# PSUM's eight banks laid out anew for the recurrence stage of a two-layer gated encoder

## The chip, the cores and the metric

One core of a Trainium2 chip runs the whole program. The metric is the device time in microseconds from launch to end, the median of several executions. The engines that matter are TensorE (PE, with its weight loads as PEld), VectorE (DVE), ScalarE (ACT), GpSimd (POOL) and the DMA queues. PSUM, into which matmuls write, has eight banks of 128 x 512 float32.

## The reference

A sequence of 512 tokens of width 1024 goes through two layers. In each, one big projection of the normalised input feeds five mixers, and a gated merge adds their outputs up:

```python
for l in range(DEPTH):
    p = jnp.einsum('bsd,dc->bsc', h, w_in[l])
    pa, pb, pc, pd, pm = split_last(p, mixer_sizes)
    o_a = mixer_dilated(pa, table_a)
    o_b = mixer_rwkv(pb, shift_mu[l], ...)        # a recurrence over 512 steps, both directions
    o_c = mixer_axial_gqa(pc, c_qnorm_g[l], c_knorm_g[l], row, col)
    o_d = mixer_diff(pd, d_lambda[l], d_subln_g[l], table_d, l)
    o_m = mixer_memory(pm, mem, w_mem_kv[l])
    y = gated_merge(h, (o_a, o_b, o_c, o_d, o_m), w_branch[l], w_gate[l], b_gate[l])
    out = jnp.einsum('bsd,de->bse', y, w_out[l])
    h = layer_norm(alpha * h + out, ln_g[l], ln_b[l])

# gated_merge: for each of the five branches i
proj = jnp.einsum('bsc,cd->bsd', o, w_branch[start:start + wdt])
gate = jax.nn.sigmoid(jnp.einsum('bsd,de->bse', h, w_gate[:, i*d:(i+1)*d]) + b_gate[i*d:(i+1)*d])
terms.append(gate * proj)
```

Four mixers are attentions. mixer_rwkv is a linear recurrence with a 64 x 64 state for each of eight heads, run forwards and backwards.

## The kernel before

All products are made in float32 as three matmuls of a high and a low part (`gemm3_steps`, L145 to L152), so a projection of one 128-wide block is 8 steps of 3 matmuls with 512 columns. Weights are loaded raw (L125) and split by ACT (L135) and DVE (L136), each part with two buffers.

A layer has three stages. In the **attention stage** (L410 to L702, SBUF pool `att`) the heads of the four attention mixers run one after the other: projections into PSUM tile pg, scores into psc, softmax on DVE and ACT, transposes into pt, the weighted sums into po, and the gate `silu2` (L347), again a projection into pg that ACT (L352) and DVE (L353) read. Finished heads are stored to DRAM (scr_o). The last PSUM read of a head is L492. In the **recurrence stage** (L705 to L1109, SBUF pool `rw`) the mixer rwkv is computed in chunks of 64 steps, for four pairs of heads and two directions: eight units, each with an `early` part (k, r and v are projected by `mixed`, L730, into pg, once for a pair; decay, masks, small products) and a `late` part (a triangular solve on DVE, L949 to L966, then the chain over the chunks, L1035 to L1043), and for a pair a `finish`, which has a `silu2` too. Before the units, `mixed` projects blocks 12 and 13. `mixed` reads its bank three times: ACT (L734), then DVE twice (L735, L736). In the **output stage** (L1112 to L1148, SBUF pool `out`) the rwkv branch is merged with gates in psc and branch products in pg, and the product with w_out and the layer norm follow.

The gates and branch products of the other four branches are **fill**: a generator (`branch_steps`, L369, through `fill`, L395) that is pulled step by step. The attention stage pulls 0.7 steps after each score of the second mixer and 0.3 after each of the last (L621, L698); the recurrence pulls one step at each of its yields (L1106), and what is left is run at its end (L1108). For one block, fill makes the gate product in a tile pf (8 steps), ACT takes its tanh (L379), the branch product goes into another tile pf (4 steps, or 2 for the last branch), and DVE multiplies (L385, or L387 and L389).

The eight banks are one pool for the whole kernel: pg two, pf one, psc two, pt two, and one for po and pm. A tile that is asked for while all banks of its name are taken waits until one has been read for the last time.

The order of the instructions on each engine is not the order of the text. A scheduler places them before the run: it prefers what stands earlier in the text, and where that isn't ready, takes later work whose inputs and buffers are. It is fixed then, and each engine works through its list in order. A pool of tiles has a beginning and an end in the text, and a pool that is opened where another was closed takes over its memory.

Of the kernel before, what the change touches and what calls it, by code (L numbers as in the profile page):

```python
# [9 lines left out]
F32 = mybir.dt.float32  # L10
# [5 lines left out]
PSUM = bass.MemoryType.PSUM  # L16
# [36 lines left out]
def encoder_kernel(ctx: ExitStack, tc: tile.TileContext, x, mem, ln_in, rel_bias, w_in, par, w_up, a_up,  # L53
# [3 lines left out]
    const = ctx.enter_context(tc.tile_pool(name="const", bufs=1))  # L57
    big = ctx.enter_context(tc.tile_pool(name="big", bufs=1))
    wp = ctx.enter_context(tc.tile_pool(name="wp", bufs=1))
    pp = ctx.enter_context(tc.tile_pool(name="pp", bufs=1, space=PSUM))  # L60

    def ps_g():
        return pp.tile([128, 512], F32, name="pg", tag="pg", bufs=2)

    def ps_f():
        return pp.tile([128, 512], F32, name="pf", tag="pf", bufs=1)

    def ps_s():
        return pp.tile([128, 512], F32, name="psc", tag="psc", bufs=2)

    def ps_t():
        return pp.tile([128, 512], F32, name="pt", tag="pt", bufs=2)

    def ps_o():
        return pp.tile([128, 512], F32, name="po", tag="pm", bufs=1)

    def ps_m():
        return pp.tile([128, 512], F32, name="pm", tag="pm", bufs=1)

    mm = nc.tensor.matmul  # L80
    act = nc.scalar.activation
    tt = nc.vector.tensor_tensor
# [89 lines left out]
    def split2(hi, lo, src, scale=None):  # L172

        if scale is None:
            nc.scalar.copy(hi, src)  # L175
            tt(lo, src, f(hi), ALU.subtract)  # L176
        else:
            act(hi, src, AF.Copy, scale=scale)
            stt(lo, src, scale, f(hi), ALU.mult, ALU.subtract)

    def rsqrt(v):


        n = v.shape[-1]
        y = wp.tile([128, 8], F32, name="rsy", tag="rsy", bufs=2)[:, :n]
        a = wp.tile([128, 8], F32, name="rsa", tag="rsa", bufs=2)[:, :n]
        ts(y.bitcast(I32), v.bitcast(I32), -0.5, float(0x5f3759df), ALU.mult, ALU.add)

        stt(a, y, 0.375 ** 0.5, v, ALU.mult, ALU.mult)
        tt(a, a, y, ALU.mult)  # L190
        stt(a, a, 1.25 / 0.375 ** 0.5, a, ALU.subtract, ALU.mult)
        stt(y, a, 1.875, y, ALU.add, ALU.mult)
        stt(a, y, -0.5, v, ALU.mult, ALU.mult)
        tt(a, a, y, ALU.mult)
        stt(v, a, 1.5, y, ALU.add, ALU.mult)
# [27 lines left out]
    def layernorm(pool, xts, gb, hT, dst):  # L223
        n = len(xts)
        mv = pool.tile([128, 4, 2], F32, name="lnmv", tag="lnmv", bufs=2)
        for j, (xt, t) in enumerate(xts):
            st = pool.tile([128, 2, 6], F32, name="lnst", tag="lnst", bufs=2)
            for i in range(2):
                nc.vector.bn_stats(out=st[:, i, :], in_=xt[:, i * 512:(i + 1) * 512])
            nc.vector.bn_aggr(out=mv[:, j], in_=st)  # L230
        ts(mv[:, :n, 1], mv[:, :n, 1], 1e-5, None, ALU.add)
        rsqrt(mv[:, :n, 1])
        for j, (xt, t) in enumerate(xts):

            for sn in (slice(0, DM),) if hT is not None else (slice(0, 512), slice(512, DM)):
                stt(xt[:, sn], xt[:, sn], mv[:, j, 0:1], gb[:, 0, sn], ALU.subtract, ALU.mult)
                stt(xt[:, sn], xt[:, sn], mv[:, j, 1:2], gb[:, 1, sn], ALU.mult, ALU.add)
                nc.sync.dma_start(out=dst[t * 128:(t + 1) * 128, sn], in_=xt[:, sn])
            if hT is None:
                continue  # L240
            for j2 in range(2):
                ps = ps_t()
                for i in range(4):
                    nc.tensor.transpose(ps[:, i * 128:(i + 1) * 128],
                                        xt[:, (4 * j2 + i) * 128:(4 * j2 + i + 1) * 128], ident)
                sl = slice(t * 128, (t + 1) * 128)
                pv = ps.rearrange("p (k t) -> p k t", k=4)
                split2(hT[:, 0, 4 * j2:4 * j2 + 4, sl], hT[:, 1, 4 * j2:4 * j2 + 4, sl], pv)
# [75 lines left out]
    for l in range(L):  # L324
# [85 lines left out]
        with tc.tile_pool(name=f"att{l}", bufs=1) as at:  # L410
# [83 lines left out]
            def gated(of, g2, out=False):  # L494
                tt(of, of, g2, ALU.mult)
                return finish_o(at, of, out)
# [29 lines left out]
            for hp in range(4):  # L526
# [21 lines left out]
                for i in range(2):  # L548
                    b = load_bias(2 * hp + i)
                    p4 = []  # L550
                    for qb in range(4):
                        ps = ps_s()
                        score(ps, q, k, i, qb, S)
                        p, _ = softmax(ps, S, b[:, 384 - 128 * qb:896 - 128 * qb])
# [55 lines left out]
            for b in range(4):  # L610
# [3 lines left out]
                for i in range(2):  # L614
                    p4 = []
                    for qb in range(4):
                        ps = ps_s()
                        score(ps, q, (kh, kl), i, qb, S, g)
                        p, _ = softmax(ps, S)
# [6 lines left out]
                t = gated(of, g2, True)  # L626
# [3 lines left out]
            with tc.tile_pool(name=f"attd{l}", bufs=1) as ad:  # L630
# [12 lines left out]
                for h in range(4):  # L643
# [23 lines left out]
                    po = ps_o()  # L667
# [9 lines left out]
                    t = finish_o(at, o, True)  # L677
# [3 lines left out]
            with tc.tile_pool(name=f"attm{l}", bufs=1) as am:  # L681
                kv = am.tile([128, 4, 256], F32, name="kvm", tag="kvm")
                nc.sync.dma_start(out=kv, in_=scr_kv[l].rearrange("b p t -> p b t"))
                for b in range(2):
# [6 lines left out]
                    for i in range(2):  # L691
                        p4 = []
                        for qb in range(4):
                            ps = ps_s()
                            score(ps, q, k, i, qb, 256)
                            p, _ = softmax(ps, 256, None, (DVE, ACT)[qb % 2])
# [4 lines left out]
                    t = gated(of, g2, True)  # L701
                    spill(4, b, t)  # L702


        with tc.tile_pool(name=f"rw{l}", bufs=1) as rp:  # L705
            def T(n, shape, bufs=1, dt=F32):
                return rp.tile(shape, dt, name=n, tag=n, bufs=bufs)
# [401 lines left out]
                pass  # L1109


        with tc.tile_pool(name=f"out{l}", bufs=1) as op:  # L1112
            yh, wo, z = [], [], []
            last = l == L - 1

            def load_z(t):
                zt = op.tile([128, DM], F32, name="z", tag="z", bufs=4)
                nc.sync.dma_start(out=zt, in_=scr_h[t * 128:(t + 1) * 128, :])
                z.append((zt, t))

            def done(db, yt):
                hi = big.tile([128, S], F32R, name="yh", tag="y", bufs=8)
                lo = op.tile([128, S], F32R, name="yl", tag="yl", bufs=8)
                split2(hi, lo, yt, 0.5)
                yh.append((hi, lo))
                t = op.tile([128, 2, DM], F32R, name="wo", tag="wo", bufs=8)
                for o in range(0, DM, 512):
                    raw = wp.tile([128, 512], F32, name="wrawr", tag="wrawr", bufs=2)
                    nc.sync.dma_start(out=raw, in_=w_out[l, db * 128:(db + 1) * 128, o:o + 512])
                    split2(t[:, 0, o:o + 512], t[:, 1, o:o + 512], raw)  # L1130
                wo.append(t)

            gb = load_gb(op, lnp[l])
            for _ in branch_steps(1, None, 4, done, "r", op, 2):
                pass
            for t in range(4):
                load_z(t)
            if not last:
                hT = new_hT()
            for t in range(4):  # L1140
                sl = slice(t * 128, (t + 1) * 128)
                for n in range(2):
                    ps = ps_g()
                    sn = slice(n * 512, (n + 1) * 512)
                    gemm3(ps, [(yh[k][0][:, sl], yh[k][1][:, sl], wo[k][:, 0, sn], wo[k][:, 1, sn]) for k in range(8)])
                    stt(z[t][0][:, sn], z[t][0][:, sn], ALPHA, ps, ALU.mult, ALU.add)
                if t:
                    layernorm(op, z[(0, 2, 3)[t - 1]:t + 1], gb, None if last else hT, out if last else scr_h)  # L1148


def _bucket(rel):
# [121 lines left out]
```

## Time and profile before

| | us |
|---|---|
| median of 3 executions (2313.76 to 2317.56) | 2314.18 |
| the profiled execution | 2311.92 |
| its span, first to last instruction | 2310.1 |

| engine | busy us | share of the span | instructions |
|---|---|---|---|
| PE (matmul) | 2206.5 | 96% | 13056 |
| PEld (weight load) | 1690.5 | 73% | 13056 |
| DVE | 1733.0 | 75% | 4236 |
| ACT | 1273.5 | 55% | 2785 |
| POOL | 60.9 | 3% | 119 |

Busy times are sums of an engine's instructions. Matmuls overlap, so a busy PE is not PE at its peak. The mean granted TensorE clock is 0.991 of full speed. In the rows below, times are microseconds from the span's start, `out<-in` names the tiles, L149 is a line of the kernel, a bracket tells how long an engine was idle before an instruction and what ended that, and a wait is put down to what came last.

### The profile page before, as it was taken

The numbers are of one execution on the slowest core, as the hardware profiler recorded it, in microseconds if no ns is written. First come the engines' busy times: TensorE is split into PE (matmuls) and PEld (weight loads), VectorE is DVE, ScalarE is ACT, GpSimd is POOL, SyncE is SP. The second block draws the span as 40 slices with busy tenths as digits, with TensorE's granted clock in tenths as the row PEclk, the third lists the DMA queues.
The fourth block names the chain that finished last, engine by engine and source line by source line (L and its number), as shares of the span: only waits on it lengthen the run. The fifth ranks groups of instructions, "written<-read, shape, count | busy, mean of one in ns | idle before, by whom it ended". The sixth has DMA issues, their size and how long they took to land.

```text
span 2310.1 us, 36289 instructions
## 1 busy us (share of the span) xinstructions
PE 2206.5 (96%) x13056; PEld 1690.5 (73%) x13056; DVE 1733.0 (75%) x4236; ACT 1273.5 (55%) x2785; POOL 60.9 (3%) x119
## 2 busy tenths in 40 slices
PE   6999999999999999999999999999999999999998
PEld 5877777777677777776877777777677777777676
DVE  7676886576889797965567778766778979878455
ACT  3555666675655565544235656666675646555440
POOL 0000000000000000000000000000000000000000
PEclk9999999999999999999999999999999999999999
DMA  7733123332222221315334321232312222222350
GB/s 261 230 95 86 64 76 96 105 95 80 73 79 70 93 77 60 108 51 190 101 116 104 94 64 62 94 99 83 114 60 92 74 65 94 72 93 67 100 180 37
DMA packets 112612, 222.58 MB, mean 96 GB/s; under 512 B 13304, under 2 KB 23288, under 8 KB 112048
## 3 DMA queue, kind: packets, MB, share of 16 engines
q1 hardware_dynamic: 102000, 196.14, 26.5%
q0 software_dynamic: 10432, 24.12, 4.1%
q8 instruction: 103, 1.69, 0.3%
q14 instruction: 77, 0.63, 0.1%
HBM read 188.71 MB, written 28.36 MB: 94 GB/s over the span
## 4 chain that ended last, share of the span: by engine, by line
PE 53%; issue 17%; DVE 17%; ACT 7%; DMA 5%; POOL 0%; SPq 0%; DVEq 0%; POOLq 0%; ACTq 0%
PE pg L150 7%; PE pg L151 7%; PE pg L149 7%; PE pf L149 5%; PE pf L150 4%; PE pf L151 4%; PE psc L443 3%; DVE pr L959 2%; DVE W L961 2%; PE po L488 2%; PE pt L469 2%; DVE wlof L136 1%; PE psc L151 1%; PE psc L150 1%; PE psc L149 1%
## 5 line engine op out<-in xcount | busy, mean ns | idle before, releaser
L150 PE MATMUL pg<-hT,whir 128*128 128x512 f32 (+1 forms) x912 | 366.0, 401 | 0.5 <-DVE hT L176 0.5
L149 PE MATMUL pg<-hT,whir 128*128 128x512 f32 (+1 forms) x912 | 364.4, 400 | 1.9 <-DVE q L424 1.6
L151 PE MATMUL pg<-hT,wlor 128*128 128x512 f32 (+1 forms) x912 | 364.3, 399 | 1.7 <-DVE wlor L136 1.7
L136 DVE TENSOR_TENSOR wlor<-wrawr,whir 128x512 fp32r<-128x512 f32 x240 | 163.7, 687 | 123.2 <-ACT whir L135 114.5
L135 ACT CAST whif<-wrawf 128x512 fp32r<-128x512 f32 (+1 forms) x272 | 164.6, 606 | 149.9 <-PE pf L150 87.4
L135 ACT CAST whir<-wrawr 128x512 fp32r<-128x512 f32 x240 | 147.5, 618 | 178.4 <-PE pg L150 111.9
L149 PE MATMUL pf<-hT,whif 128*128 128x512 f32 x512 | 223.0, 435 | 8.9 <-DVE y L385 5.0
L136 DVE TENSOR_TENSOR wlof<-wrawf,whif 128x512 fp32r<-128x512 f32 (+1 forms) x272 | 181.6, 669 | 48.3 <-ACT whif L135 43.1
L150 PE MATMUL pf<-hT,whif 128*128 128x512 f32 x512 | 208.3, 407 | 0.0
L151 PE MATMUL pf<-hT,wlof 128*128 128x512 f32 x512 | 207.7, 406 | 0.0
L151 PEld LDWEIGHTS pg<-hT,wlor 128*128 128x128 f32 x912 | 172.2, 189 | 40.6 <-DVE wlor L136 4.2
L149 PEld LDWEIGHTS pg<-hT,whir 128*128 128x128 f32 x912 | 172.4, 189 | 38.8 <-ACT whir L135 2.6
L150 PEld LDWEIGHTS pg<-hT,whir 128*128 128x128 f32 x912 | 172.2, 189 | 37.8 <-issue 3.6
L176 DVE TENSOR_TENSOR pT<-pt,pT 128x512 fp32r<-128x512 f32 x176 | 114.2, 686 | 36.3 <-ACT pT L175 34.9
L175 ACT CAST pT<-pt 128x512 fp32r<-128x512 f32 x176 | 94.6, 588 | 63.7 <-PE pt L469 62.6
L149 PEld LDWEIGHTS pf<-hT,whif 128*128 128x128 f32 x512 | 97.5, 190 | 41.2 <-DVE gt L387 10.7
L469 PE MATMUL pt<-cst,p 128*128 128x128 f32 x704 | 118.6, 273 | 0.0
L151 PEld LDWEIGHTS pf<-hT,wlof 128*128 128x128 f32 x512 | 97.3, 190 | 22.4 <-issue 1.6
L959 DVE TENSOR_TENSOR pr<-W,U 128x60 f32<-128x60 f32 (+24 forms) x496 | 103.8, 209 | 11.9
L150 PEld LDWEIGHTS pf<-hT,whif 128*128 128x128 f32 x512 | 98.0, 191 | 18.9 <-issue 3.9
L961 DVE TENSOR_TENSOR W<-W,pr 128x60 f32<-128x60 f32 (+24 forms) x496 | 102.8, 207 | 10.8
L469 PEld LDWEIGHTS pt<-cst,p 128*128 128x128 f32 x704 | 89.7, 141 | 27.3 <-DVE p L460 2.9
(324 smaller groups left out, 4836.9 us busy)
## 6 DMA issues: line engine op xcount, KB each, us to landing
wrawr<-in_w_in_dram SPq DMA_DIRECT2D x224, 256.0 KB, 2.8
wrawf<-in_w_gate_dram SPq DMA_DIRECT2D x160, 256.0 KB, 2.8
o<-scr_o POOLq DMA_DIRECT2D x28, 512.0 KB, 4.5
wrawf<-in_w_branch_dram SPq DMA_DIRECT2D x48, 256.0 KB, 2.7
bias<-scr_toe SPq DMA_DIRECT2D x24, 448.0 KB, 3.3
scr_o<-os SPq DMA_DIRECT2D x20, 512.0 KB, 3.1
wrawf<-in_w_in_dram SPq DMA_DIRECT2D x32, 256.0 KB, 3.2
wrawr<-in_w_out_dram SPq DMA_DIRECT2D x32, 256.0 KB, 3.0
```

The costliest lines, as they stand in the source:

```text
L135: nc.scalar.copy(hi, raw)
L136: tt(lo, raw, f(hi), ALU.subtract)
L149: mm(ps, ah, bh, start=(i == 0), stop=False)
L150: mm(ps, ah, bl, start=False, stop=False)
L151: mm(ps, al, bh, start=False, stop=(i == n - 1))
L175: nc.scalar.copy(hi, src)
L176: tt(lo, src, f(hi), ALU.subtract)
L443: mm(ps[:, :nk], q[:, i, sl], part[:, i if g is None else g, :nk], start=(j == 0), stop=(j == 1))
L469: nc.tensor.transpose(pt[:, qb * 128:(qb + 1) * 128], p4[qb][:, kb * 128:(kb + 1) * 128], ident)
L488: mm(po, vwin(kb), pT[:, b, :], start=(kb == 0 and b == 0), stop=(kb == nkb - 1 and b == 1))
L959: tt(pr, W[:, t8, s:s + 1].to_broadcast([128, nt, n]), U[:, s:s + 1, rsl].to_broadcast([128, nt, n]), ALU.mult)
L961: tt(W[:, t8, rsl], W[:, t8, rsl], pr, ALU.add)
```

## The change

The single PSUM pool becomes a sequence of pools, closed and opened by a helper `banks`. Around the recurrence of each layer the layout is pg one, pf two; before it and after it, pg two and pf one, as it was. psc, pt and the bank for po and pm keep their numbers. The functions that hand out tiles (`ps_g`, `ps_f` and the others) take them from the pool that is open when they are called. The generator of the fill is not touched: it is resumed under whichever pool is open.

```diff
@@ -57,26 +57,38 @@
     const = ctx.enter_context(tc.tile_pool(name="const", bufs=1))
     big = ctx.enter_context(tc.tile_pool(name="big", bufs=1))
     wp = ctx.enter_context(tc.tile_pool(name="wp", bufs=1))
-    pp = ctx.enter_context(tc.tile_pool(name="pp", bufs=1, space=PSUM))
+
+    pool = {}
+
+    def banks(name, **bufs):
+
+        if pool:
+            pool["p"].__exit__(None, None, None)
+        pool["p"] = tc.tile_pool(name=name, bufs=1, space=PSUM)
+        pool["t"], pool["n"] = pool["p"].__enter__(), bufs
+
+    def ps_of(tag, name):
+        return pool["t"].tile([128, 512], F32, name=name, tag=tag, bufs=pool["n"][tag])
 
     def ps_g():
-        return pp.tile([128, 512], F32, name="pg", tag="pg", bufs=2)
+        return ps_of("pg", "pg")
 
     def ps_f():
-        return pp.tile([128, 512], F32, name="pf", tag="pf", bufs=1)
+        return ps_of("pf", "pf")
 
     def ps_s():
-        return pp.tile([128, 512], F32, name="psc", tag="psc", bufs=2)
+        return ps_of("psc", "psc")
 
     def ps_t():
-        return pp.tile([128, 512], F32, name="pt", tag="pt", bufs=2)
+        return ps_of("pt", "pt")
 
     def ps_o():
-        return pp.tile([128, 512], F32, name="po", tag="pm", bufs=1)
+        return ps_of("pm", "po")
 
     def ps_m():
-        return pp.tile([128, 512], F32, name="pm", tag="pm", bufs=1)
-
+        return ps_of("pm", "pm")
+
+    banks("pp", pg=2, pf=1, psc=2, pt=2, pm=1)
     mm = nc.tensor.matmul
     act = nc.scalar.activation
     tt = nc.vector.tensor_tensor
@@ -702,6 +714,7 @@
                     spill(4, b, t)
 
 
+        banks(f"pr{l}", pg=1, pf=2, psc=2, pt=2, pm=1)
         with tc.tile_pool(name=f"rw{l}", bufs=1) as rp:
             def T(n, shape, bufs=1, dt=F32):
                 return rp.tile(shape, dt, name=n, tag=n, bufs=bufs)
@@ -1109,6 +1122,7 @@
                 pass
 
 
+        banks(f"pp{l}", pg=2, pf=1, psc=2, pt=2, pm=1)
         with tc.tile_pool(name=f"out{l}", bufs=1) as op:
             yh, wo, z = [], [], []
             last = l == L - 1
@@ -1146,6 +1160,7 @@
                     stt(z[t][0][:, sn], z[t][0][:, sn], ALPHA, ps, ALU.mult, ALU.add)
                 if t:
                     layernorm(op, z[(0, 2, 3)[t - 1]:t + 1], gb, None if last else hT, out if last else scr_h)
+    pool["p"].__exit__(None, None, None)
 
 
 def _bucket(rel):
```

## Rows read from the trace of the kernel before

**Rows 1.** Stages: busy us (instructions) of PE, PEld, DVE, ACT, POOL; clock; DMA.
```profile
506.00:528.00 22.00, 21.31 (x110) 16.39 (x109) 18.31 (x46) 17.97 (x48) 0.00 (x0) 1.00 0.21 73
541.00:1057.00 516.00, 499.10 (x3699) 373.24 (x3698) 419.21 (x1132) 293.14 (x698) 7.02 (x13) 0.99 0.24 75
1667.00:2184.00 517.00, 500.19 (x3704) 374.27 (x3703) 420.78 (x1136) 294.78 (x700) 7.02 (x13) 0.99 0.24 75
```

**Rows 2.** Timeline of PE, two matmuls in a row: start, duration, line, tiles.
```profile
540.05 0.39 PE L150 MATMUL pg<-hT,whir 128*128 128x512 f32 x1
540.28 0.39 PE L151 MATMUL pg<-hT,wlor 128*128 128x512 f32 x1
```

**Rows 3.** Waits of PE, 541 to 1057: total us, times, longest.
```profile
PE pt L1031 <- DVE PE L1023: 2.9, 4, 0.9
PE pf L149 <- ACT gt L379: 2.9, 6, 0.8
PE pt L977 <- DVE U L973: 2.7, 2, 1.9
PE pf L149 <- DVE gt L387: 1.6, 4, 0.8
PE psc L788 <- ACT tmp L785: 1.2, 1, 1.2
```

**Rows 4.** Waits of the weight loads, 541 to 1057.
```profile
PEld pf L149 <- ACT gt L379: 8.6, 19, 1.1
...
PEld pf L149 <- DVE gt L387: 5.3, 12, 1.2
```

**Rows 5.** Timeline of PE where attention ends.
```profile
529.83 0.50 PE L149 MATMUL pf<-hT,whif 128*128 128x512 f32 x1 [2.52 <-DVE y L385]
...
530.41 0.63 PE L151 MATMUL pf<-hT,wlof 128*128 128x512 f32 x1
...
538.31 0.50 PE L149 MATMUL pf<-o,whif 128*128 128x512 f32 x1 [1.07 <-ACT gt L379]
```

**Rows 6.** Stage 506 to 527.8, instructions of tile pg, then of pf.
```profile
506.00:527.80 21.80, 14.26 (x46) 7.95 (x45) 0.69 (x1) 0.61 (x1) 1.00 0.21 73
506.00:527.80 21.80, 1.89 (x6) 1.12 (x6) 0.00 (x0) 0.00 (x0) 1.00 0.21 73
```

**Rows 7.** Timelines of ACT and DVE at the seams.
```profile
475.27 0.70 ACT L379 ACTIVATE gt<-pf,hb 128x512 f32<-128x512 f32 x1
...
508.34 0.69 DVE L353 SCALAR_TENSOR_TENSOR g<-g,pg 128x512 f32<-128x512 f32 x1
...
527.04 0.69 DVE L492 SCALAR_TENSOR_TENSOR of<-po,olo 64x512 f32<-64x512 f32 x1 [1.30 <-ACT olo L491]
...
535.51 0.17 DVE L715 TENSOR_TENSOR cf<-par 128x14 f32<-128x14 f32 x1
...
1054.62 0.68 DVE L353 SCALAR_TENSOR_TENSOR g<-g,pg 128x512 f32<-128x512 f32 x1
...
1056.67 0.69 DVE L387 SCALAR_TENSOR_TENSOR gt<-gt,pf 128x512 f32<-128x512 f32 x1 [0.64 <-PE pf L151]
```

**Rows 8.** Waits of all engines, 535 to 1025.
```profile
POOL WD L724 <- DMA scr_o<-os: 34.8, 1, 34.8
```

**Rows 9.** Timeline of PE, first matmuls of the output stage.
```profile
1026.06 0.40 PE L149 MATMUL pg<-o,whir 128*128 128x512 f32 x1
...
1052.76 0.50 PE L149 MATMUL psc<-hT,whif 128*128 128x512 f32 x1 [0.78 <-ACT whif L135]
```

**Rows 10.** Timeline of PE in the output stages of both layers.
```profile
1069.29 0.50 PE L149 MATMUL pg<-o,whir 128*128 128x512 f32 x1 [3.21 <-DMA o<-scr_o]
...
2197.56 0.79 PE L149 MATMUL pg<-o,whir 128*128 128x512 f32 x1 [5.18 <-DMA o<-scr_o]
```

**Rows 11.** Timelines of ACT and DVE, reads of a k projection.
```profile
545.88 0.68 ACT L734 ACTIVATE k<-pg,cf 128x512 f32<-128x512 f32 x1
...
547.40 0.75 DVE L736 SCALAR_TENSOR_TENSOR k<-pg,par,k 128x511 f32<-128x511 f32 x1
```

## Prediction

> **What bounds the kernel now.** I read the stages first [rows 1]. In the two recurrence stages (541 to 1057 and 1667 to 2184 us) rows of PE matmuls cover 97% of the time (499.1 of 516.0), those of DVE 81% and of ACT 57%; the granted clock is 0.99 of the full 2.4 GHz. Matmul rows overlap, so their pitch tells more: two 512-column matmuls start 0.23 us apart [rows 2], though each row says 0.39. PE's queue is in order, so whatever waits at its head delays all behind it. Next I read what PE waits for in a recurrence [rows 3]. The five longest lines sum to 11.3 us of 516, and the two that name tile pf to 2.9 + 1.6 = 4.5: pf is one bank, so a gate product has to be read by the tanh on ACT (L379) before the branch product may start in it, and that one by DVE (L387) before the next gate. The weight loads of the same two waits show 8.6 + 5.3 = 13.9 us [rows 4], but a weight load can wait while the matmul ahead of it still streams, so that is a ceiling. No line of PE's waits in the recurrence is a wait for a bank of pg: two banks do for the projections today.
>
> Then the seams. Where attention ends and the recurrence begins, PE is full until 527.3 us, stands 2.52 us before the next gate (until L385 has read pf), runs some 8 matmuls at the lower clock level of 1.2 GHz (rows of 0.63 instead of 0.39) and stands another 1.07 us on pf [rows 5]; layer 1 repeats the pattern. What keeps it full before: from 506 to 527.8 us it runs 46 recorded matmuls into pg and 6 into pf [rows 6]. The last attention read of pg is L353 at 508.34 [rows 7], so nearly all of the 46 are the recurrence's first two projections (blocks 12 and 13, 2 x 8 x 3 = 48 by the code), placed between the last softmax steps, and the six are half of a branch product that the text pulls only later. Work of the recurrence fills PE while the tail of attention goes through ACT and DVE.
>
> **Part one: two banks for pf.** The 4.5 us of pf waits go. Next behind them is the split of the weights (L135, L136), which has no pf line among PE's five longest. Between 4.5 (PE's rows) and 13.9 (weight loads) I take 5.5, near the lower end, since a late weight load costs only what the matmul ahead of it doesn't cover. The stalls at the seam belong to the next part.
>
> **Part two: the seam into the recurrence.** To close one PSUM pool and open another is more than new names. The kernel already does it with SBUF (att, then rw, then out), and the trace shows the price: the first writes of rw's tiles, WD on POOL and cf on DVE, come only when the last store out of an att tile (scr_o<-os) is done; POOL waits 34.8 us for that, and cf, which reads only par, starts at 535.51 [rows 8]. I take it that a PSUM pool behaves alike: no matmul into the recurrence's banks before the last attention bank is read (L492, 527.04 + 0.69 = 527.7 us [rows 7]) and before the one gate product begun in the old pool is finished. (The attention part pulls 32 x 0.7 + 16 x 0.3 = 27.2 steps, so the text leaves the third gate after 3 of 8; the trace has it read by the tanh at 475.3 [rows 7], so the bank read at 527.7 decides.) The 48 projection matmuls and the 12 of the third branch product, all ahead of that point now, have to come behind it: 60 x 0.232 = 13.9 us of PE work. Something comes back. Without them the tail of attention is shorter, but it is a chain over ACT and DVE, which are busy 18.0 and 18.3 of its 22 us [rows 1]: at most 22 - 18.3 = 3.7 us, and some 1.2 us more from the PE-bound stretch before it, which the other 6 of the 12 leave (6 x 0.232 = 1.4). Of these 4.9 I take 3. And the two stalls on pf behind the seam go, 2.52 + 1.07 = 3.6 us, since there are a second bank and the deferred work to run. Net 13.9 - 3 - 3.6 = +7.3 us a layer, between 13.9 - 4.9 - 3.6 = +5.4 and 13.9 - 3.6 = +10.3. The stretch at 1.2 GHz, some 8 x 0.2 us, I leave in: PE stands ahead of the seam then as it stands behind it now.
>
> **Part three: the seam out of the recurrence.** Today 14 matmuls of the output stage (8 into psc, 6 into pg, the first at 1026) run before 1055.3 us, when L353 has read the recurrence's last bank [rows 9]; the last read of pf, by L387, is at 1057.4, and 6 more have run by then. Behind a barrier they come later: 14 to 20 x 0.232 = 3.2 to 4.6 us. But at 1066 us PE stands 3.21 us (5.18 in layer 1, at 2192) for the reload of o, which hangs on the recurrence's last result and not on PE [rows 10]. The delay goes into that stall: I take 0, with -1 (the stretch at 1.2 GHz behind the stall goes) and +3 (the weights of this stage are split later too) as ends.
>
> **Part four: one bank for pg.** A projection's bank is free after one ACT and two DVE passes; the first k projection is read from 545.88 to 548.15, 2.3 us with the queueing between [rows 11]. In a layer's recurrence 2 + 12 + 4 = 18 tiles go through pg (lower ranks, k/r/v of four pairs, gates). In those 2.3 us PE may run fill or recurrence work: there are 341 fill steps a layer (96 x 3 + 80 = 368, less 27), 3 matmuls each. If one is always ready the cost is zero, if none is it is 18 x 2.3 = 41 us. The nearest row is pf's own: some 56 hand-overs of a single bank between 541 and 1057 (two for each of 28 pairs of products) cost PE 4.5 us, 0.08 each, behind one reader. For three passes in two queues I take 2 to 3 times that, 0.2 x 18 = +3.5.
>
> By the Trainium skill's Perfetto Trace Analysis (Matmuls) independent groups should rotate through different PSUM banks, so that the reading of one overlaps the next one's matmuls. For pf the rows agree; for pg the rule speaks against the change, and by it the sum would be that of the last rival below.
>
> **Sum.** -5.5 + 7.3 + 0 + 3.5 = +5.3 us a layer; the layers' rows are alike (516 and 517 us), so +10.6, say 10. The profiled execution took 2311.92 us (span 2310.1 and 1.8 around it), 2.3 under the median of three, 2314.18. The profile would go to some 2322, the median to **2324**.
>
> **Rivals.** First, faster: there is no such barrier, or one for each bank alone. Then the recurrence's projections still start in the tail, part two keeps only its gain (-3.6) and part three is 0: -5.5 - 3.6 + 3.5 = -5.6 a layer, 2303. It decides where the first matmul into a recurrence tile stands: ahead of L492 or behind it. For it: PSUM tiles of one bank each, so a narrower rule is conceivable. Against it: [rows 8].
>
> Second, no change that can be told: the barrier is there at its lower end (+5.4), pf gives 7 to 8 (between 4.5 and 13.9), the hand-overs cost 3: within 1 us a layer, 2314.
>
> Third, slower by more: the single pg bank stretches the recurrence's opening. The first eviction can't begin before rw's tiles may be written (535.5), and block 13, k, r and v then follow at 5.6 + 2.3 us each, the last ending at about 538 + 5.6 + 3 x 7.9 = 567, some 11 us later than today's 556.5. Fill runs in the gaps, but is then missing at the recurrence's end, where the last unit's chain through DVE stands uncovered. It decides where the recurrence can't make up the delay, and DVE at 81% leaves little room. Up to 11 more a layer, half of it made up: 5.3 + 6 to 11, about +14 a layer, 2342.
>
> Last, every hand-over at its full price: 41 instead of 3.5 us a layer, 2 x 37.5 more than the forecast, 2399. No pg wait in today's rows points there, and fill is at hand; I count it in the third with 2 in 100.
>
> **How the numbers follow.** Forecast (2319 to 2331) 0.41, slower by more 0.19, faster (2296 to 2309) 0.22, no change 0.18. About 0.2%, 4.6 us, is what a measurement of this kernel can tell from no change; so faster 0.22, same 0.18, slower 0.60. The range for 8 in 10 takes in the middle of the first rival and of the third: 2302 to 2342. The forecast's own range is 2319 to 2331.
>
> **What would show it.** In the profile after: no PE line pf <- ACT gt or pf <- DVE gt or y (part one); between some 506 and 527 us hardly a pg matmul, a PE share near a half, and the first matmul of the recurrence right behind L492 (part two); a shorter wait for o (part three); lines pg <- DVE k, r, v of some 3 us a layer (part four). I am wrong if projections of blocks 12 and 13 run ahead of L492, if the tail of attention shrinks by over 5 us, or if pg's waits sum to over 10 us a layer.

## The result, and the profile after

The changed kernel takes 2357.5 us (median; 2356.6 to 2359.7), the kernel before beside it 2315.9: ratio 1.0182, 95% interval 1.0164 to 1.0199, so 42 us slower. The sign was forecast, the size (+10) was not, and the time lies outside the range (2302 to 2342). The profiled execution has a span of 2356.2 us at a mean granted clock of 0.975 (before 2310.1 at 0.991). Lines of the new file stand 12 or 13 further down: the matmuls of a projection, L149 to L151, are L161 to L163, `mixed`'s three reads, L734 to L736, are L747 to L749.

The same 13056 matmuls take 2234.3 us of rows instead of 2206.5, and PE stands without one for 121.9 us (2356.2 - 2234.3) instead of 103.6. So 28 of the 46 us between the two spans are rows that got longer, as they do at the lower clock level (0.63 instead of 0.39 us in the timeline below), and 18 are standing.

Stages of the changed kernel, columns as in [rows 1]:

```profile
506.00:528.00 22.00, 16.76 (x60) 10.83 (x59) 15.42 (x43) 14.93 (x42) 0.00 (x0) 0.71 0.10 36
528.00:541.00 13.00, 11.59 (x38) 9.03 (x38) 5.41 (x15) 3.47 (x7) 1.24 (x3) 0.70 0.19 69
541.00:1078.00 537.00, 513.77 (x3741) 391.12 (x3739) 428.93 (x1143) 300.52 (x707) 7.04 (x13) 0.97 0.24 74
```

In the tail of attention 60 matmuls are left of 110, at a clock of 0.71 instead of 1.00. The recurrence (541 to 1078) takes 537 us instead of 516 and holds 42 matmuls more (3741 against 3699), which at 0.232 us each are some 10 of the 21 us. PE's timeline at the seam answers [rows 5]:

```profile
525.87 2.37 PE L500 MATMUL po<-pT,v 128*128 128x512 f32 x4 [0.46 <-ACT pT L187]
529.65 0.79 PE L161 MATMUL pg<-hT,whir 128*128 128x512 f32 x1 [1.41 <-DVE of L504]
530.24 0.63 PE L162 MATMUL pg<-hT,whir 128*128 128x512 f32 x1
...
535.36 0.58 PE L162 MATMUL pg<-hT,whir 128*128 128x512 f32 x1
535.78 0.39 PE L163 MATMUL pg<-hT,wlor 128*128 128x512 f32 x1
```

The barrier is there, and where it was forecast: the recurrence's first matmul waits for L504, the old L492, the last attention read of PSUM. It then runs six microseconds of longer rows (0.63 instead of 0.39 us, starting 0.43 apart instead of 0.23). That last read has itself moved, to 528.90 us from 527.04 [rows 7]. PE's waits in the recurrence, 541 to 1078, answer [rows 3]:

```profile
PE psc L890 <- DVE pr L972: 4.3, 1, 4.3
PE pm L104 <- DVE W L974: 2.6, 1, 2.6
...
PE pg L161 <- DVE k L749: 1.3, 1, 1.3
...
PE pf L161 <- ACT gt L391: 1.1, 2, 0.6
```

The waits on pf are nearly gone (4.5 before), as forecast. The waits on pg are 1.3 us. Nothing in this list is as large as the 16 us a layer by which the time exceeds the forecast (21 against 5.3), and that is the lesson of the case: the price of a scarce bank need not stand in the waits that name it.

### The profile page after: what moved, and what is told of

Its sections match the earlier page's. It is cut to its first block, busy times and chain, and to the rows that moved or that the text cites. A ratio compares the mean times of both kernels' runs of the same rounds, so it can differ in the third digit from the quotient of the medians.

```text
span 2356.2 us, 36296 instructions
## 1 busy us (share of the span) xinstructions
PE 2234.3 (95%) x13056; PEld 1720.8 (73%) x13056; DVE 1740.6 (74%) x4236; ACT 1278.2 (54%) x2785; POOL 61.5 (3%) x119
## 4 chain that ended last, share of the span: by engine, by line
PE 47%; issue 25%; DVE 17%; ACT 7%; DMA 4%; POOL 1%; SPq 0%; DVEq 0%; POOLq 0%; ACTq 0%
PE pg L161 6%; PE pg L162 6%; PE pg L163 6%; PE pf L161 4%; PE pf L163 3%; PE pf L162 3%; DVE W L974 2%; DVE pr L972 2%; PE psc L455 2%; PE po L500 1%; DVE wlof L148 1%; PE psc L161 1%; PE pt L481 1%; PE psc L163 1%; PE psc L162 1%
## 5 line engine op out<-in xcount | busy, mean ns | idle before, releaser
L161 PE MATMUL pg<-hT,whir 128*128 128x512 f32 (+1 forms) x912 | 365.0, 400 | 9.0 <-DVE of L504 2.8
L163 PE MATMUL pg<-hT,wlor 128*128 128x512 f32 (+1 forms) x912 | 364.5, 400 | 1.5 <-DVE wlor L148 1.5
L161 PE MATMUL pf<-hT,whif 128*128 128x512 f32 x512 | 222.1, 434 | 2.2 <-ACT gt L391 2.2
L161 PEld LDWEIGHTS pg<-hT,whir 128*128 128x128 f32 x912 | 173.5, 190 | 52.3 <-ACT whir L147 5.0
L163 PE MATMUL pf<-hT,wlof 128*128 128x512 f32 x512 | 210.0, 410 | 0.8 <-DVE wlof L148 0.8
L163 PEld LDWEIGHTS pg<-hT,wlor 128*128 128x128 f32 x912 | 173.4, 190 | 42.9 <-DVE wlor L148 5.5
L161 PEld LDWEIGHTS pf<-hT,whif 128*128 128x128 f32 x512 | 98.3, 192 | 26.9 <-issue 4.7
L163 PEld LDWEIGHTS pf<-hT,wlof 128*128 128x128 f32 x512 | 98.1, 192 | 24.3 <-issue 1.9
L972 DVE TENSOR_TENSOR pr<-W,U 128x60 f32<-128x60 f32 (+24 forms) x496 | 103.6, 209 | 12.8
L162 PEld LDWEIGHTS pf<-hT,whif 128*128 128x128 f32 x512 | 98.6, 193 | 19.4 <-issue 3.7
```

Of the source, the lines that this page charges most:

```text
L161: mm(ps, ah, bh, start=(i == 0), stop=False)
L162: mm(ps, ah, bl, start=False, stop=False)
L163: mm(ps, al, bh, start=False, stop=(i == n - 1))
L972: tt(pr, W[:, t8, s:s + 1].to_broadcast([128, nt, n]), U[:, s:s + 1, rsl].to_broadcast([128, nt, n]), ALU.mult)
```

## The experiments

All ratios are against the kernel before, run beside each kernel on the same chip. "Standing" is the span less PE's rows, both from the page of the profiled execution.

| kernel | seam in / out | pg, pf in the recurrence | ratio (95%) | span | standing |
|---|---|---|---|---|---|
| before | - | 2, 1 | 1 | 2310.1 | 103.6 |
| changed | both | 1, 2 | 1.0182 (1.0164 to 1.0199) | 2356.2 | 121.9 |
| seams alone | both | 2, 1 | 1.0103 (1.0081 to 1.0126) | 2340.6 | 114.1 |
| first seam alone | in | 2, 1 | 1.0070 (1.0049 to 1.0091) | 2332.0 | 111.4 |
| second seam alone | out | 2, 1 | 1.0033 (1.0023 to 1.0043) | 2319.7 | 114.3 |
| fixed turn, control | - | 2, 1 | 0.9984 (0.9972 to 0.9996) | 2305.7 | 101.2 |
| layout alone | - | 1, 2 | 1.0047 (1.0029 to 1.0065) | 2324.6 | 108.9 |
| one pg, one pf | - | 1, 1 | 1.0101 (1.0075 to 1.0127) | 2336.1 | 123.5 |
| one pg in the opening only | - | 1 then 2, 1 | 1.0002 (0.9992 to 1.0012) | 2313.2 | 107.8 |
| one pg behind the opening only | - | 2 then 1, 1 | 1.0086 (1.0071 to 1.0101) | 2334.3 | 124.8 |

### The seams

The kernel with the seams alone has the helper `banks` and both switches, with the old numbers:

```diff
+        banks(f"pr{l}", pg=2, pf=1, psc=2, pt=2, pm=1)
         with tc.tile_pool(name=f"rw{l}", bufs=1) as rp:
...
+        banks(f"pp{l}", pg=2, pf=1, psc=2, pt=2, pm=1)
         with tc.tile_pool(name=f"out{l}", bufs=1) as op:
```

> Both switches of the change stand here, but each opens the layout of before again (two pg banks, one pf), so only the seams are new. Seam theory: the 42 us of the change lie in the seams, in the 60 deferred products, the stretch at 1.2 GHz beside them and the fill that is out of its place afterwards; this kernel is then 30 to 45 us slower than before (ratio 1.013 to 1.020). Bank theory: the single pg bank costs most of it, by projections that wait for a bank and fill that is spent too early; this kernel is then 10 to 15 us slower (1.004 to 1.006), which is what the prediction gave the first seam.

It measured +24 us, between the two theories. The next has only the first of the two switches, the one after it only the second.

> Only the switch ahead of the recurrence, to the layout of before; its pool then stays open to the next layer's recurrence. Seam theory: the first seam is the larger part, 22 to 32 us slower than before (1.0095 to 1.014), and the rest up to the kernel with both switches is the seam out of the recurrence, some 10 us. Bank theory: 8 to 12 us slower, and the seam out costs nothing.

> Only the switch behind each recurrence, to the layout of before; none ahead of it. The prediction's step: nothing, -1 to +3 us a layer, since the delay goes into the wait for o (0.999 to 1.0025). By the difference of the two kernels with one and with both seams: 8 us slower (1.002 to 1.005), because PE's queue is in order and the matmuls held back stand behind the wait for o as well.

The first seam costs 0.0070 x 2314 = 16.2 us, **8.1 a layer** (forecast 7.3, between 5.4 and 10.3): that step held. The second costs 7.6 us, **3.8 a layer**, where the forecast was nothing, at most 3. The two add up to the kernel with both (0.0103). PE of the kernel with the second seam alone, against [rows 9, 10]:

```profile
1055.29 0.50 PE L161 MATMUL pf<-o,whif 128*128 128x512 f32 x1 [1.61 <-ACT gt L391]
1058.73 0.47 PE L161 MATMUL psc<-hT,whif 128*128 128x512 f32 x1 [1.76 <-ACT yhi L1093]
1072.41 0.80 PE L161 MATMUL pg<-o,whir 128*128 128x512 f32 x1 [5.53 <-DMA o<-scr_o]
```

The output stage starts at 1058.73 instead of 1026, and the wait for o is not shorter but longer, 5.53 instead of 3.21. Ahead of that wait 34 matmuls of the stage have run, in the kernel before 52. PE's queue is in order: the 18 that are missing don't slip into the wait, they stand behind it, 18 x 0.232 = 4.2 us.

### The layout without a seam

One pool stays open with a tag for every bank, and pg and pf take theirs in a fixed turn:

```diff
+    turn = {"g": 0, "f": 0, "rec": False}
+    def bank(name, which, tags):
+        turn[which] += 1
+        return pp.tile([128, 512], F32, name=name, tag=tags[turn[which] % len(tags)], bufs=1)
     def ps_g():
+        return bank("pg", "g", ("pg",) if turn["rec"] else ("pg", "ps"))
     def ps_f():
+        return bank("pf", "f", ("pf", "ps") if turn["rec"] else ("pf",))
```

`turn["rec"]` is true from the start of a recurrence to its end. In the kernel with one pg and one pf bank "ps" lies idle there, in the control it stays with pg.

> The new layout without a seam: one pool stays open, its eight banks have a tag each, and in the recurrence one of pg's two banks is handed to pf; no bank is ever given back between stages. Seam theory: within 5 us of before on either side (0.998 to 1.002). Bank theory: 25 to 35 us slower (1.011 to 1.015).

> No seam; in the recurrence pg has one bank and pf one, so the bank taken from pg lies idle. Seam theory: 0 to 8 us slower than before (1.000 to 1.0035), the prediction's 3.5 us a layer at most. Bank theory: 30 to 40 us slower (1.013 to 1.017), since nothing is given back by pf.

> Control for the kernels without a seam: one pool, the layout of before in every stage, only that the banks of pg are handed out in a fixed turn from two tags. Both theories: within 0.2% of before. What it differs by is to be taken off the other kernels without a seam.

The fixed turn alone is worth -4 us, so 0.9984 is the base of this group. Taking pg's second bank away costs 1.0101 - 0.9984 = 0.0117, 27 us, **13.5 a layer** (10 to 17 by the two intervals; forecast 3.5). Giving it to pf brings 1.0101 - 1.0047 = 0.0054 back, 12.5 us, **6 a layer** (2.6 to 9.9; forecast 5.5). Neither theory was right alone: 8.1 + 3.8 + 13.5 - 6 = 19.4 a layer, 39 of the 42 us. One of the four steps was sized four times too small. That the four add up so well is in part luck, since they overlap (see below). With one bank each for pg and pf, PE's timeline shows it standing where the second unit begins:

```profile
605.90 1.19 PE L884 MATMUL psc<-AR,BK 64*128 64x128 f32 x4 [5.87 <-DVE pr L966]
...
611.88 1.08 PE L918 MATMUL psc<-cst,tmp 128*128 128x128 f32 x4 [2.08 <-DVE W L968]
```

The waiting instruction is the first small product of the second unit, and what it waits for is DVE, not a bank.

### Where the single bank costs: attempts that failed

I first held that block 12's bank is the trouble. It can't be read before rw's tiles may be written (535 us [rows 8]), so with one bank block 13 can't be placed in attention's tail. In the first two runs pg's second bank is handed to pf later, behind the first pair's k, r and v, or behind blocks 12 and 13.

```diff
                     up, k, r, v = res
+                    turn["rec"] = True
```

> No seam; pg's second bank goes to pf only when the first pair's projections k, r and v have been placed; from there to the end of the recurrence pg has one bank and pf two, as in the change. Opening theory: the single pg bank costs its 10 to 12 us a layer in the opening alone, where the bank of block 12 can't be read before rw's tiles may be written (535 us), and later hand-overs are hidden by fill; then only the gain of pf's second bank is left, 5 us a layer, and the time is 6 to 12 us under that of before (0.995 to 0.9975). Hand-over theory: each of the 18 hand-overs costs its part, 0.6 us; 5 of the 18 are taken away, and the time is 0 to 8 us above before (1.000 to 1.0035).

> As the run before it, but pg's second bank goes to pf already behind blocks 12 and 13, ahead of the first pair's k, r and v. If the cost of the opening is that block 12's bank is blocked until 535 us, and block 13 can't be placed in the tail of attention, it is gone here too: 6 to 12 us under before (0.995 to 0.9975). If it is the three hand-overs from k to r to v at 2.3 us each, most of it is still here: 3 us under to 6 us above (0.999 to 1.0025).

They measured 1.0098 (1.0082 to 1.0115) and 1.0121 (1.0108 to 1.0134), worse than handing it over at once (1.0047). A row of each tells why, the first of the one with the bank handed over behind k, r and v, the second of the other:

```profile
541.92 0.77 PE L155 MATMUL pg<-hT,whir 128*128 128x512 f32 x1 [11.70 <-DVE tmp L742]
```

```profile
538.48 0.77 PE L155 MATMUL pf<-hT,whif 128*128 128x512 f32 x1 [11.60 <-DVE tmp L742]
```

The edit made a new stall: fill that is given the shared bank can't start before a projection there has been read, and the fill that covered 530 to 542 is gone. These two tell nothing of the question. In the next two cf and the tile for block 12 lie outside rw, so that its bank is read in attention's tail; the second is the control with two pg banks.

```diff
-                cf = T("cf", [128, 42])
+                cf = big.tile([128, 42], F32, name="cf", tag="cf", bufs=1)
...
-                    t = tmp()
+                    t = tmp() if b else big.tile([128, S], F32, name="tmp", tag="low", bufs=1)
```

> The kernel without a seam and with the new layout (one pg bank, two pf), but cf and the tile that block 12 is read into lie outside rw (oraw of attention has one buffer instead of two to make room), so that block 12's bank can be read in the tail of attention and block 13 be placed there, as with two banks. Blocked-bank theory: the single bank costs because block 12 holds it until rw's tiles may be written; now the first k projection comes as early as before (within 3 us, instead of 9.8 us later), and the time falls from 1.0047 to 0.993 to 0.999. Hand-over theory (k to r to v): the first k early, v late, and the time stays at 1.003 to 1.006.

> Control: the kernel of the fixed turn (two pg banks, one pf, no seam) with the same three tiles moved. Block 12's bank is free earlier here too, so k can start some 3 us earlier; both theories: 0.994 to 0.9995 of before, within 0.3% of the fixed turn alone.

1.0048 (1.0035 to 1.0060) and 0.9931 (0.9918 to 0.9943). In the first, block 12 is read at 521.98 and the first k at 544.37, as early as before, and the time is that of the layout alone (1.0047). The layout of one pg and two pf banks now costs 0.0117, 27 us, over its control, where without the move it costs 1.0047 - 0.9984 = 0.0063, 15 us: the move helps the control and not the single bank. The simple form of the theory falls. The control, by the way, is 16 us faster than the kernel before.

In two more, work is moved into the holes. The changed kernel with more fill pulled in the last attention block (`pull(2.91 if b else 0.3)`), and with 32 useless matmuls a layer behind attention:

```diff
+                dummy = ps_g()
+                for n in range(32):
+                    mm(dummy, q[:, n % 2, 0:128], q[:, n % 2, :], start=True, stop=True)
```

> The changed kernel; only that the last attention block pulls 2.91 instead of 0.3 fill steps at each of its 8 places, 48 in all, four whole pairs of products: 21 steps, 62 matmuls, 14.4 us of PE, move from the recurrence into the tail that the seam had emptied. If the hole in the tail is what the seam costs (idle PE and the lower clock behind it): granted clock in 506 to 528 near 1, and 7 to 12 us a layer come back, 1.0182 against before falls to 1.008 to 1.012. If it is the order of the recurrence's opening, it stays at 1.016 to 1.018.

> The changed kernel with 32 useless matmuls more in each layer, placed last in the attention stage, on q of its last block, into a pg bank that nobody reads: 7 us of PE at 2.4 GHz and nothing for any other engine. By the sum over rows, 32 of the change's 46 us are matmuls at 1.2 GHz. If the emptied tail's low clock costs by itself (tail 3 us longer than it need be, 23 matmuls behind the seam at double pitch), the kernel gets faster by work added: 3 to 6 us a layer less, 1.013 to 1.0155. If not, the added work costs 0 to 3 us a layer, 1.018 to 1.021.

(Of the 46 us between the spans 28 are longer rows, as the page gives them, not the 32 of the second expectation.) The first measured 1.0186 (1.0171 to 1.0202), no gain, though the row of its tail shows PE nearly full at full clock:

```profile
506.00:528.00 22.00, 20.14 (x108) 15.23 (x107) 20.04 (x54) 19.77 (x54) 0.00 (x0) 1.00 0.24 81
```

Three rows of PE's timeline in its recurrence:

```profile
609.12 1.13 PE L890 MATMUL psc<-AR,BK 64*128 64x128 f32 x7 [2.40 <-DVE pr L972]
623.87 0.80 PE L161 MATMUL pf<-hT,whif 128*128 128x512 f32 x1 [2.15 <-ACT whif L147]
644.15 0.31 PE L990 MATMUL pt<-U,NS 32*32 32x32 f32 x2 [3.27 <-DVE U L986]
```

The changed kernel stands longer at the first of these places (4.3, in the list above), but not at the second, and 0.65 us at the third. The fill is a fixed amount: what the tail takes is missing later. That this makes the two new stops is my reading. The second kernel measured 1.0167 (1.0142 to 1.0191); the interval overlaps the changed kernel's, so no verdict on the time. Its first two stages, columns as in [rows 1]:

```profile
506.00:528.00 22.00, 19.81 (x96) 13.79 (x94) 16.97 (x46) 16.54 (x46) 0.00 (x0) 0.94 0.10 36
528.00:541.00 13.00, 11.59 (x39) 9.08 (x38) 5.65 (x15) 3.71 (x7) 1.24 (x3) 0.71 0.21 75
```

The clock in the tail rose from 0.71 to 0.94 and the matmuls behind the seam didn't get any faster (39 recorded, 38 without). Of a price of the tail's low clock itself the run shows nothing beyond its interval.

### Where it costs: opening or later

The kernel with one pg and one pf bank, with the second pg bank returned behind the first pair's projections, and its complement (`turn["rec"] = p < 3` at the same place, false ahead of it):

> No seam, one bank for pf throughout; pg has one bank from the start of each recurrence until the first pair's k, r and v are placed, and two again from there on. Compared with the control of the fixed turn (0.9984). Opening theory: most of the 27 us by which the single bank costs over the control arises here, 0.9984 rises to 1.004 to 1.008. Theory of the later stages: 5 of 18 hand-overs, the rest being the later pairs and the way into the output stage: 0.999 to 1.002.

> The complement: no seam, one bank for pf; pg has two banks through the opening, one from there until the last pair's k, r and v are placed, then two again, so that the output stage finds both. Opening theory: within 2 us a layer of the control (0.9984 to 1.000). Theory of the later stages: 4 to 8 us a layer (1.002 to 1.005). What is left to the kernel with one pg bank throughout (1.0101) is the price of the way into the output stage.

Against the control's 0.9984 the opening alone costs 0.0018, 4 us, **2 a layer**; the rest alone 0.0102, 24 us, **12 a layer**; together 28, against 27 for one bank throughout. By that sum nothing would be left for the way into the output stage, but the traces show a price there. Ahead of PE's wait for o 52 matmuls of the output stage run in the control, 41 in the kernel with one pg bank throughout and 34 in the one with the layout alone, as many as with the second seam. And of the 30.4 us between the spans of the kernel with one bank throughout and the control, 11.2 have arisen by ACT's read of the last pair's result in layer 0, 9.2 arise in the recurrence of layer 1, and 10 behind the two. So the layout alone already costs part of what the second seam costs, the two parts overlap, and the sums of 28 and of 39 us hide it. ACT's reads of r of the second pair and of the finished last pair, in the control and then in the kernel with one bank behind the opening:

```profile
605.83 0.69 ACT L741 ACTIVATE r<-pg,cf 128x512 f32<-128x512 f32 x1
...
1055.42 0.62 ACT L1088 CAST yhi<-ys 128x512 fp32r<-128x512 f32 x1
```

```profile
626.79 0.69 ACT L740 ACTIVATE r<-pg,cf 128x512 f32<-128x512 f32 x1
...
1069.14 0.61 ACT L1088 CAST yhi<-ys 128x512 fp32r<-128x512 f32 x1
```

r comes 21.0 us late and the layer's recurrence ends 13.7 us late; up to the second pair's k the two differ by 0.4 us. So the delay begins at the second pair. The kernel before shows what is special there, ACT's reads of its k and r, DVE's two reads of the same k, and the stage around them, columns as in [rows 1]:

```profile
593.25 0.68 ACT L734 ACTIVATE k<-pg,cf 128x512 f32<-128x512 f32 x1
607.08 0.69 ACT L734 ACTIVATE r<-pg,cf 128x512 f32<-128x512 f32 x1
...
610.46 0.74 DVE L735 SCALAR_TENSOR_TENSOR k<-pg,par,k 128x511 f32<-128x511 f32 x1
612.31 0.74 DVE L736 SCALAR_TENSOR_TENSOR k<-pg,par,k 128x511 f32<-128x511 f32 x1
...
588.00:613.00 25.00, 23.58 (x147) 17.85 (x147) 23.69 (x72) 16.01 (x43) 0.00 (x0) 1.00 0.16 49
```

Its bank is held from 593.25 to 613.05, **19.8 us** from ACT's read on, not 2.3: DVE is busy 23.69 of the 25 us, with the first unit's solve among other work, and comes to it late. Before the change the second bank takes r meanwhile (607.08). In the changed kernel k is held as long and r has to wait:

```profile
605.26 0.67 ACT L747 ACTIVATE k<-pg,cf 128x512 f32<-128x512 f32 x1
635.75 0.68 ACT L747 ACTIVATE r<-pg,cf 128x512 f32<-128x512 f32 x1
...
603.60 0.68 DVE L847 TENSOR_TENSOR tmp<-tmp,k 128x512 f32<-128x512 f32 x1
...
624.35 0.74 DVE L748 SCALAR_TENSOR_TENSOR k<-pg,par,k 128x511 f32<-128x511 f32 x1
625.14 0.74 DVE L749 SCALAR_TENSOR_TENSOR k<-pg,par,k 128x511 f32<-128x511 f32 x1
```

ACT is late there too. The last matmul into this bank ends at 590.9, but the SBUF tile k has one buffer, and DVE reads the first pair's k for the last time at 603.60 (L847). A second buffer for k was not tried.

That the held bank makes the 12 us is argued from these rows, not shown, and others speak against it as the whole cause. In the kernel with the seams alone, which has two pg banks, the second pair's k is read at 593.70 and its r at 631.75, later than the 626.79 above. And in the kernel with one pg bank in the opening only, r is 22.4 us late and the recurrence ends only 6.7 us late:

```profile
628.27 0.69 ACT L741 ACTIVATE r<-pg,cf 128x512 f32<-128x512 f32 x1 [0.91 <-PE pg L157]
...
1062.12 0.62 ACT L1089 CAST yhi<-ys 128x512 fp32r<-128x512 f32 x1
```

### Is it the fill, or the time a bank is held?

With one pg and one pf bank, 183 fill matmuls have started by the first read of k, in the control 138: fill runs ahead in the projections' place. If that were the harm, useless matmuls there would help. 48 a layer, on `lowr`, into pm, ahead of `project`:

> The kernel with one pg and one pf bank and no seam; 48 useless matmuls more in each layer (11 us of PE), on the lower ranks of block 12, into a bank of its own, placed ahead of the first pair's projections. They can run while the projections wait for their bank, in the place of the 48 fill matmuls that run there ahead of their turn. If fill spent early is what costs (the holes of 5.9 and 2.1 us at 606 and 612 and the 17 us at 1.2 GHz behind them), the kernel gets faster by work added: from 1.0101 to 1.002 to 1.007. If the late k, r and v cost by themselves, it stays or gets slower: 1.010 to 1.018.

1.0148 (1.0130 to 1.0166) instead of 1.0101: 11 us slower. All 48 ran between 536 and 566 us, and the first k is read at 562.29 instead of 555.51. But they took the place of 12 fill matmuls only: 171 have started by the first read of k, still 33 more than in the control. So work added here doesn't help; whether fill that runs early is the harm, the run doesn't tell.

Then the holding. `mixed` copies its bank in one ACT pass, and the three reads go to the copy:

```diff
-                    act(dst, ps, AF.Copy, scale=cf[:, blk:blk + 1])
+                    c = T("mx", [128, S], 2)
+                    nc.scalar.copy(c, ps)
+                    act(dst, c, AF.Copy, scale=cf[:, blk:blk + 1])
...
-                    stt(dst[:, 1:], ps[:, :S - 1], P("mu0", blk), dst[:, 1:], ALU.mult, ALU.add)
+                    stt(dst[:, 1:], c[:, :S - 1], P("mu0", blk), dst[:, 1:], ALU.mult, ALU.add)
```

> The changed kernel, seams and all, with the same copy. Hold theory: the 12 us a layer of the later hand-overs go but for some 2, and 1.0182 falls to 1.008 to 1.012, near the kernel with the seams alone (1.0103) less the gain of pf's second bank. Other theories: 1.016 to 1.021.

> Control: the fixed turn with two pg banks and the same copy. 14 ACT passes of 0.7 us a layer are added, 10 us on an engine that is 57% busy; the pair of k can also start earlier. All theories: 0.995 to 1.003 of before.

> One pg bank and one pf bank in the recurrence, no seam, and each of the 14 mixed projections of a layer (two lower ranks, k, r, v of four pairs) copied from its bank by ACT in one pass, into one of two SBUF tiles, from which the three passes of before then read. Hold theory: the bank is dear because DVE reads it late (the second pair's k is read by ACT at 593.2 and by DVE at 612.3, 19.8 us, not the 2.3 us of the first pair); freed after one ACT pass, the single bank costs no more than 4 us a layer over the control with the same copy (0 to 8 us, instead of 27 without the copy). Other theories (the order of the fill, the late first projections): the 27 us stay, within 5.

| | without the copy | with it | gained |
|---|---|---|---|
| changed kernel | 1.0182 | 1.0035 (1.0022 to 1.0048) | 34 us |
| two pg, one pf, no seam | 0.9984 | 0.9919 (0.9906 to 0.9932) | 15 us |
| one pg, one pf, no seam | 1.0101 | 1.0046 (1.0032 to 1.0061) | 13 us |

The changed kernel wins 34 of its 42 us back by 14 added ACT passes a layer, 19 more than the control does. Its second k, as before read late by DVE (616.16, 619.17), now leaves the bank at once, and r still comes 33 us behind it:

```profile
597.25 0.56 ACT L748 COPY mx<-pg 128x512 f32<-128x512 f32 x1
630.38 0.58 ACT L748 COPY mx<-pg 128x512 f32<-128x512 f32 x1
...
616.16 0.74 DVE L750 SCALAR_TENSOR_TENSOR k<-mx,par,k 128x511 f32<-128x511 f32 x1
619.17 0.74 DVE L751 SCALAR_TENSOR_TENSOR k<-mx,par,k 128x511 f32<-128x511 f32 x1
```

But the third line contradicts the simple reading: with one pf bank the single pg bank still costs 29 us over its control, where the hold theory had at most 8. ACT's copies of the lower ranks and the last pair's result, in the control (both copies in one row) and in the kernel with one bank (its second copy):

```profile
532.81 1.08 ACT L742 COPY mx<-pg 128x512 f32<-128x512 f32 x2
...
1047.71 0.61 ACT L1090 CAST yhi<-ys 128x512 fp32r<-128x512 f32 x1
```

```profile
541.01 0.58 ACT L742 COPY mx<-pg 128x512 f32<-128x512 f32 x1
...
1055.49 0.62 ACT L1090 CAST yhi<-ys 128x512 fp32r<-128x512 f32 x1 [0.53 <-DVE ys L1088]
```

Block 13 is read some 7.7 us late (541.01 against about 533.3, the second half of the row), the second pair's k 4.0 us (590.59 against 586.59), and the recurrence ends 7.8 us late; in layer 1 it is 7.3, 3.6 and 8.8 us, counted from the read of block 12. So half of the late opening is made up by the second pair, and as much is lost again behind it. The rest of the 26.4 us between the two spans, 10 us, lies behind the recurrences, where 39 instead of 51 matmuls of the output stage run ahead of the wait for o. The copy empties the bank at once and the price stays: the time that the bank is held is not the whole cause, and what is stays open. The layout of one pg and two pf banks with the copy and no seam was not run.

## Why the prediction was wrong, step by step

- **What bounds the kernel** held, with one gap: the second pair of projections, where DVE is full, was not looked at. [rows 11] is a row of the first pair, in an opening in which DVE has little else to do. And that no wait named a bank of pg didn't tell what the second bank was worth.
- **Part one**, two banks for pf, -5.5 a layer: -6 measured, and the pf waits fell from 4.5 to 1.1 us. Right, as far as an interval of 2.6 to 9.9 tells.
- **Part two**, the seam in, +7.3: +8.1 measured, first matmul right behind the last attention read. Right in sum. In detail the tail did not get 3 us shorter (its last PSUM read comes at 528.90 instead of 527.04, and cf is written 0.5 us later than before). That the sum came out near the forecast is in part luck.
- **Part three**, the seam out, 0 (-1 to +3): +3.8. Wrong: "the delay goes into that stall" needs work that can pass the stalled instruction, and PE's queue is in order. The layout without a seam holds back 18 matmuls as well.
- **Part four**, one bank for pg, +3.5: +13.5. This is the step that failed. The term was 18 hand-overs x 0.2, as if all were alike; the 0.2 came from pf's hand-overs, and the 2.3 us from the first pair. Measured, the opening with 5 of the 18 costs 2 us a layer and what comes behind it 12, beginning at the second pair, whose k holds its bank 19.8 us. Size and place are shown by runs. That the holding makes the 12 is not: the copy ends it and leaves the price at 29 us with one pf bank, so the cause stays open. The end of the range (41) did contain it; I took a value near the other end and then gave that case 2 in 100. The third rival named the opening, which costs only 2 us a layer by itself.
- "I am wrong if pg's waits sum to over 10 us a layer": they sum to 1.3, and the step was wrong all the same. The scheduler fixes the order with the bank's scarcity in it, so that PE, as I read it, meets the lateness elsewhere: psc <- DVE pr 4.3, pm <- DVE W 2.6, and rows at 1.2 GHz.
- **The clock**, "some 8 x 0.2 us, I leave in": a mean of 0.975 instead of 0.991, with levels 1.0 and 0.5, means that some 118 us of 2356 ran at 1.2 GHz (2 x 0.025 x 2356) instead of 42. PE's rows grew by 28 us with it. I read it not as a cost beside the four steps but as the second payment for each hole: once standing, once behind it.

The steps, as measured alone, sum to 39 of 42 us, within their intervals; but the layout and the second seam each hold back 18 matmuls of the output stage, and both together hardly more (19), so the sum counts them twice and something else makes up for it. Open is what makes the 13.5 us of the single bank, and why it costs as much with the copy.

The fastest kernel here is a by-product: the fixed turn with the copy, 0.9919 of before (2295 us); cf and the tile for block 12 outside rw (and one buffer instead of two for oraw) give 0.9931 without it.

## What to carry to other kernels

Price a bank over all places where it is used, up to its last reader's end, and not by the first row found: here it is held 2.3 us at one place and 19.8 at another. Then test the price with a run, since here neither the waits that name the bank (1.3 us) nor the longest hold accounts for the 13.5 us a layer. If the reader is late, one cheap pass that empties the bank can be worth more than a second bank, as in the changed kernel (34 us, against 18 between it and the seams alone), or less, as with one bank each (13 against 27). And work that is held back in front of a stall doesn't use the stall if the queue is in order.

## What the runs showed of the hardware

The granted clock of TensorE fell without a long stop. In the changed kernel's tail of attention the longest stop between two matmul rows is 1.16 us (at 524.7), PE's rows still cover 16.76 of 22 us, and the clock is 0.71; with 21.31 of 22 it is 1.00 [rows 1]. It falls twice: it is 0.50 of full speed from 512 to 514 us, 1.00 from 516 to 518 and 0.50 again from 520 on, and ahead of the two falls no stop is longer than 0.84 us. The low level then holds for some 6 us of dense matmuls behind the seam. The Trainium skill's TensorE: Matmul & The Clock Gate (A second HAM failure mode: psum-queue depth-cycling) tells of a kernel whose short pauses between groups of matmuls were enough to make the clock swing between its two levels; this case's rows agree.

The Trainium skill's Perfetto Trace Analysis (Matmuls), by which groups of matmuls should rotate through banks, pointed the right way for pg: by that rule the prediction had its last rival, 2399, and the single bank cost 27 us of the 82 (2 x 41) that it would have at full price.
